# A hybrid decoder layer on one core: the first pair's upper norm factor and seeds earlier, its gate weights split later, the gates' copies one unit later, and the index matrix in another tile

## Chip, core and metric

The kernel runs on one core of one Trainium2 chip. The metric is the device time of one execution in microseconds, the median of several runs. The engines are TensorE (PE, with its weight loads PEld), VectorE (DVE), ScalarE (ACT), GpSimd (POOL) and SyncE (SP); nearly all DMAs are issued by SP, in the order of its queue.

## What is computed

One layer for x of 512 rows by 2048 columns, in float32:

```python
h = rms_norm(x, norm1_g)
proj = h @ w_in            # q, k, v, r of four GLA heads; a rank-16 gate ga; q, k, v of eight dilated heads
gate_pre = ga @ gla_gate_w2 + gla_gate_b
log_g = log_sigmoid(gate_pre) / 16
out_a = gla_mixer(qa, ka, va, ra, log_g)          # chunked gated linear attention
out_b = dilated_mixer(qb, kb, vb, rel_bias)       # three dilated branches, T5 bias by distance
x = x + concat(out_a, out_b) @ w_out
h2 = rms_norm(x, norm2_g)
x = x + (silu(h2 @ w_gate) * (h2 @ w_up)) @ w_down
```

## The kernel before

**Products.** All large matrix products are done as Strassen-like products: two neighbouring 512-column blocks of a weight are a pair, and a pair takes seven products (P1 to P7) of sums of quarters instead of eight. Each operand is split into a high float32r part and a low remainder, and three of the four cross terms are multiplied. For the weights ACT makes the high part (a cast to tile `wh`) and VectorE the low one (a subtraction to `wl`); VectorE also makes the sums of quarters (`wa`, `wb` with `wc`, `wd`). One block is 8 matmuls of 128x512 with the high weight and 4 with the low one; a pair of the input projection has seven products of four blocks, 0 to 27. `wh` and `wl` have two buffers each, the quarters 12, the results that are gathered in SBUF (tag C: seeds and outputs) six, and there are four accumulators and four further PSUM banks.

**The first pair** (q and k of the GLA heads; function `first_pair`) is not left to the scheduler. The string PLAN is a list of tokens, one step each, and the engines execute their instructions in the order of the tokens. The tokens that matter here: `h.k` and `l.k` are the high and low part of weight block k (line 519 on ACT, 527 on VectorE); `mH.k` and `mL.k` (`mH2`, `mL2` for a second result) its high and low matmuls (line 474); `+W.k` a sum of weight quarters (514); `x` scales the transposed input, `+S`, `hi` and `lo` make sums of its quarters and their two parts (494, 504, 208, 211). `sq` squares a half row tile of x with a row sum (681), and `nA.half`, `nB.half`, `nC.half` make the norm factor of the upper (0) or lower (1) 256 rows from these sums: two VectorE instructions (691, 692), a logarithm and an exponential on ACT (694, 695), and three more on VectorE (697 to 699). `seedX.m` copies an accumulator that will be overwritten to a tile of tag C (542), `closeX.m` adds the other part (545), and `sclX.m` multiplies by the norm factor (550); after the second `scl` of a result its two tiles are stored (1065). The results are a, b, c and d: eight tiles, so seedd takes the buffers of seeda after their stores. `gp`, `gh.i` and `gl.i` prepare the rank-16 gate weights: GpSimd sums them (724 to 726), ACT makes the high part (737) and VectorE the low one; `rank` multiplies them (760).

**The next pair** (v of the GLA heads, accumulators at line 402, parts at 373 and 377, sums at 298) goes through Tile's scheduler, with background work: after the matmuls of a block, `step` advances a list of generators by one unit. The first is `gates`, then `bias_tables`; the GLA heads follow when their columns of v are there. In `gates` the 16-row gate product is copied and loaded four times (774, 777), it and the second gate weight are split (779 to 789), and for each of the four row tiles a matmul (795) is scaled and biased by VectorE (797), put through a log-sigmoid (801 to 804) and stored to ls_d (805). `bias_tables` loads a 33x640 matrix of bucket indices in two parts (662), multiplies each with the bias table (664), copies the result (666), stores it (667), and replicates it 128 times in DRAM (669). A `work` tile has one buffer for each tag: a new use of the tag waits until the earlier use has ended. Tag v holds a gate row between 797 and 804, PT the second gate weight, oT the gate bias until the fourth row has read it. A GLA head loads ls_d to T (822), multiplies it for the cumulative sums (833, 834), takes exponentials on ACT (836 to 844), transposes q and k (849), scales them on VectorE (853 to 862), and multiplies them for the scores (873).

Of the kernel before, what the change touches and what calls it, by code (L numbers as in the profile page):

```python
# [20 lines left out]
D = 2048  # L21
# [4 lines left out]
NB = 640  # L26
# [44 lines left out]


PLAN = """
D.r11.3 D.a.3 D.r21.3 D.r12.3 D.c.3 D.r22.3 D.a.0 D.r11.0 D.r11.1 D.a.1 D.a.2 D.r11.2 D.r12.0
D.c.0 D.r12.1 D.r12.2 D.c.1 D.r21.0 D.r22.0 D.b.0 D.c.2 D.r21.1 D.r22.1 D.b.1 D.r22.2 D.r21.2
D.d.0 D.gw D.b.2 x.r11.3.0 x.r11.3.1 hi.A11.3 h.0 lo.A11.3 x.r21.3.0 l.0 mH.0 D.d.1 D.row.0.1
D.row.0.0 D.row.2.0 D.row.1.1 D.row.1.0 D.row.2.1 x.r21.3.1 x.r12.3.1 hi.A21.3 x.r12.3.0 lo.A21.3
h.1 x.r22.3.1 l.1 D.d.2 D.row.3.0 D.row.3.1 D.sm mL.0 hi.A12.3 x.r22.3.0 lo.A12.3 hi.A22.3 +S1.3
x.r11.0.1 mH2.0 x.r11.1.1 lo.A22.3 x.r11.1.0 x.r11.0.0 hi.A11.1 mL2.0 h.2 lo.A11.1 mH.1 hi.A11.0
l.2 x.r11.2.0 x.r11.2.1 mL.1 lo.A11.0 x.r12.0.0 x.r12.0.1 hi.A11.2 mH2.1 hi.A12.0 lo.A11.2  # L80
hi.S1.3 lo.A12.0 x.r12.1.1 mL2.1 lo.S1.3 x.r12.2.0 h.3 +S2.3 mH.2 +S3.3 x.r12.2.1 x.r12.1.0 l.3
hi.A12.2 mL.2 h.4 lo.A12.2 mH.3 hi.A12.1 l.4 x.r21.0.0 x.r22.0.0 +W.8 x.r22.0.1 mL.3 x.r21.0.1
h.5 mH.4 +S1.0 lo.A12.1 x.r21.1.1 hi.S1.0 l.5 mL.4 x.r22.1.0 h.6 lo.S1.0 mH.5 +W.9 x.r22.1.1
x.r21.2.1 x.r22.2.0 l.6 mL.5 x.r22.2.1 h.7 mH.6 gp +S2.0 seeda.0 l.7 x.r21.1.0 seeda.1 mL.6 +W.10
h.8 mH.7 gh.1 +S1.1 hi.S2.0 l.8 x.r21.2.0 hi.S1.1 mL.7 h.9 +S1.2 mH.8 +W.11 hi.S1.2 gh.0 hi.A22.2
lo.S1.1 mL.8 sq.0.1 lo.S1.2 mH.9 l.9 h.10 lo.S2.0 hi.A22.1 sq.1.1 mL.9 +W.12 mH.10 h.11 +S2.1
l.10 hi.S2.1 sq.1.0 l.11 mL.10 h.12 mH.11 lo.S2.1 seedb.0 closea.0 seedb.1 l.12 hi.A22.0 mL.11
sq.3.0 closea.1 mH.12 gl.0 sq.2.1 gl.1 +W.13 hi.S2.3 mL.12 +S2.2 h.14 rank.0 +S3.0 hi.S2.2 l.14
h.13 lo.S2.2 sq.3.1 l.13 sq.0.0 +S4.0 mH.13 hi.S3.0 +S3.2 hi.S4.0 +S3.1 sq.2.0 lo.S4.0 mL.13
+S4.1 h.15 mH.14 +S4.2 hi.S4.1 lo.A22.0 seedc.1 lo.S4.1 mL.14 hi.S4.2 l.15 h.16 mH.15 lo.S4.2  # L90
seedc.0 l.16 mL.15 lo.A22.1 mH.16 lo.A22.2 hi.S3.2 +W.17 mL.16 +W.19 h.17 rank.1 lo.S3.0 lo.S3.2
hi.S3.1 +W.22 l.17 mH.17 +W.18 D.d.3 D.b.3 lo.S3.1 h.18 mL.17 +W.21 h.19 mH.18 l.18 hi.S3.3 l.19
mL.18 mH.19 +W.20 nA.1 h.20 lo.S2.3 mL.19 lo.S3.3 h.21 mH.20 l.20 nB.1 l.21 mL.20 h.22 +S4.3
mH.21 nC.1 l.22 mL.21 h.23 nA.0 mH.22 nB.0 l.23 nC.0 mL.22 h.24 mH.23 scla.0 l.24 scla.1 mL.23
seedd.0 seedd.1 closed.0 mH2.23 closed.1 scld.0 scld.1 mL2.23 h.25 mH.24 hi.S4.3 l.25 lo.S4.3
mL.24 mH2.24 closec.0 closec.1 sclc.0 sclc.1 mL2.24 closeb.1 sclb.1 closeb.0 sclb.0
"""


# [32 lines left out]
def block_kernel(ctx: ExitStack, tc: tile.TileContext, ins, out):  # L132
    nc = tc.nc
    x, w_in, w_out, w_gate, w_up, w_down = (
        ins[n] for n in ("x", "w_in", "w_out", "w_gate", "w_up", "w_down")
    )
# [15 lines left out]
    def nm(s):  # L152
        uid[0] += 1
        return f"{s}_{uid[0]}"
# [499 lines left out]
    def bias_tables():  # L654


        rel = work("T", (33, 8))
        nc.gpsimd.memset(rel[32:33, :], 1.0)
        load(rel[0:32, :], ins["rel_bias"])
        for c0, cn, t0, t1 in ((0, 512, "v", "qT"), (512, NB - 512, "oT", "kT")):  # L660
            oh = work(t0, (33, cn))
            load(oh, ins["onehot"][:, c0 : c0 + cn])
            bp = bank()
            nc.tensor.matmul(bp[:8, :cn], rel, oh, start=True, stop=True)
# [4 lines left out]
        load(rep_d, bass.AP(tensor=bias_d.tensor, offset=0, ap=[[NB, 8], [0, P], [1, NB]]))  # L669
        yield  # L670
# [46 lines left out]
    rank = {}  # L717
# [48 lines left out]
    def gates():  # L766
# [20 lines left out]
        for i in (32, 96):  # L787
            r = slice(i, i + 32)
            nc.vector.tensor_tensor(
                gas[r, :], ga4[r, :], gas[r, :].bitcast(F32), op=ALU.subtract  # L790
            )
        yield
        for t in range(4):
            zp = bank()
# [749 lines left out]
```

## Time and profile before

| | |
|---|---|
| median of three runs | 1941.62 us (1940.41 to 1941.84) |
| the profiled execution | 1938.88 us |
| its span | 1937.1 us |
| granted TensorE clock, mean | 0.999 |
| busy in the span: TensorE, weight loads | 1918.9, 1662.9 us |
| VectorE, ACT, GpSimd | 1650.3, 1094.8, 16.8 us |
| instructions | 25614 |

A row of the timeline gives the start and the length in us, engine, line, operation, result and operands, sizes and the number of instructions merged into it; in brackets stands how long the engine was idle before and what released it. SPq is SP's queue of DMA issues; the length there is that of the issuing, not of the transfer. Ends of matmuls are modelled, and a matmul row overlaps the next one a little.

### The profile page before, as it was taken

The page shows a single profiled execution, that of the slowest core. Times are in us where ns is not written, and L with a number is a line of the kernel's source. Part 1 is how long each engine was busy: PE and PEld are TensorE (multiplying, and loading weights), DVE is VectorE, ACT ScalarE, POOL GpSimd, SP SyncE. Part 2 cuts the span into 40 slices and gives each one's busy share as a digit, 9 for nine tenths or more (in the row PEclk, how much of TensorE's full clock was granted, in tenths as well). Part 3 has the DMA queues.
Part 4 walks back from the last instruction along what each step waited for, and adds up shares of the span by engine and source line. Part 5 has one row for each costly group of instructions (what it writes and reads, how often), then busy time and mean ns, then how long its engine had stood idle before and what let it go on. Part 6 is the DMA issues. An engine that isn't in the chain of part 4 may idle for free.

```text
span 1937.1 us, 25614 instructions
## 1 busy us (share of the span) xinstructions
PE 1918.9 (99%) x9178; PEld 1662.9 (86%) x9178; DVE 1650.3 (85%) x1936; ACT 1094.8 (57%) x1634; POOL 16.8 (1%) x25
## 2 busy tenths in 40 slices
PE   9999999999999999999999999999999999999999
PEld 7888888888888888888888888888888888888887
DVE  8896887778799999878878878878879989989987
ACT  9564564667766675544544545544546646546443
POOL 1000100000000000000000000000000000000000
PEclk9999999999999999999999999999999999999999
DMA  8536555444536564455454454453555865855762
GB/s 337 195 109 220 168 180 173 140 157 146 185 131 208 177 213 130 136 180 161 137 180 156 138 185 142 152 185 122 172 169 175 292 210 184 297 190 180 244 218 66
DMA packets 150360, 345.75 MB, mean 178 GB/s; under 512 B 15494, under 2 KB 42671, under 8 KB 150232
## 3 DMA queue, kind: packets, MB, share of 16 engines
q1 hardware_dynamic: 149944, 343.98, 52.9%
q8 instruction: 72, 1.18, 0.3%
q14 instruction: 56, 0.46, 0.1%
q10 hardware_dynamic: 288, 0.14, 0.0%
HBM read 286.10 MB, written 60.31 MB: 179 GB/s over the span
## 4 chain that ended last, share of the span: by engine, by line
PE 87%; DVE 6%; DMA 4%; issue 2%; ACT 1%; SPq 0%; POOL 0%; DVEq 0%; ACTq 0%; POOLq 0%
PE acc L402 79%; DVE wl L377 2%; PE acc L474 2%; PE bank L1078 1%; PE bank L987 1%; PE bank L963 1%; DVE wa L298 1%; PE bank L980 0%; DVE AS L199 0%; DMA T<-in_xt 0%; DMA k<-in_gw 0%; PE bank L760 0%; DMA wb<-in_w_in 0%; PE bank L954 0%; PE bank L474 0%
## 5 line engine op out<-in xcount | busy, mean ns | idle before, releaser
L402 PE MATMUL acc<-wh,AS 128*128 128x512 f32 x3008 | 711.8, 379 | 0.0
L402 PEld LDWEIGHTS acc<-wh,AS 128*128 128x128 f32 x3008 | 568.2, 189 | 81.2 <-ACT wh L373 0.5
L373 ACT CAST wh<-wa 128x1024 fp32r<-128x1024 f32 x376 | 394.3, 1049 | 396.3 <-PE acc L402 367.6
L402 PE MATMUL acc<-wh,AA 128*128 128x512 f32 x2256 | 534.7, 380 | 0.5 <-ACT wh L373 0.5
L377 DVE TENSOR_TENSOR wl<-wa,wh 128x1024 fp32r<-128x1024 f32 x376 | 456.7, 1217 | 73.0 <-ACT wh L373 47.3
L402 PEld LDWEIGHTS acc<-wh,AA 128*128 128x128 f32 x2256 | 427.1, 189 | 61.7 <-ACT wh L373 0.9
L402 PE MATMUL acc<-wl,AS 128*128 128x512 f32 x1504 | 393.8, 384 | 1.8 <-DVE wl L377 1.6
L402 PEld LDWEIGHTS acc<-wl,AS 128*128 128x128 f32 x1504 | 280.0, 189 | 51.4 <-DVE wl L377 10.2
L402 PE MATMUL acc<-wl,AA 128*128 128x512 f32 x1128 | 296.4, 385 | 0.2
L402 PEld LDWEIGHTS acc<-wl,AA 128*128 128x128 f32 x1128 | 209.9, 189 | 31.4 <-DVE wl L377 2.4
L373 ACT CAST wh<-wb 128x1024 fp32r<-128x1024 f32 x94 | 98.6, 1049 | 123.6 <-PE acc L402 118.9
L373 ACT CAST wh<-wc 128x1024 fp32r<-128x1024 f32 x94 | 98.5, 1048 | 115.9 <-PE acc L402 107.8
L373 ACT CAST wh<-wd 128x1024 fp32r<-128x1024 f32 x94 | 98.6, 1049 | 102.2 <-PE acc L402 98.6
L377 DVE TENSOR_TENSOR wl<-wc,wh 128x1024 fp32r<-128x1024 f32 x94 | 114.5, 1219 | 40.4 <-ACT wh L373 40.4
L377 DVE TENSOR_TENSOR wl<-wd,wh 128x1024 fp32r<-128x1024 f32 x94 | 114.4, 1219 | 36.5 <-ACT wh L373 29.6
L298 DVE TENSOR_TENSOR wa<-wc,wa 128x1024 f32<-128x1024 f32 x94 | 114.4, 1219 | 32.9 <-DMA wc<-in_w_gate 22.1
L377 DVE TENSOR_TENSOR wl<-wb,wh 128x1024 fp32r<-128x1024 f32 x94 | 114.0, 1216 | 5.0 <-ACT wh L373 4.8
L298 DVE TENSOR_TENSOR wa<-wb,wa 128x1024 f32<-128x1024 f32 x94 | 113.6, 1218 | 1.2 <-DMA wb<-in_w_in 0.5
L298 DVE TENSOR_TENSOR wb<-wd,wb 128x1024 f32<-128x1024 f32 x94 | 114.0, 1216 | 0.4
L298 DVE TENSOR_TENSOR wa<-wd,wa 128x1024 f32<-128x1024 f32 x94 | 112.9, 1215 | 0.1
L340 DVE SCALAR_TENSOR_TENSOR seed<-acc,rs,seed 128x512 f32<-128x512 f32 x96 | 70.4, 745 | 29.4 <-PE acc L402 29.3
L324 ACT ACTIVATE seed<-acc,rs 128x512 f32<-128x512 f32 x96 | 60.6, 682 | 5.0 <-PE acc L402 4.9
(320 smaller groups left out, 1315.5 us busy)
## 6 DMA issues: line engine op xcount, KB each, us to landing
wa<-in_w_gate SPq DMA_DIRECT2D x44, 512.0 KB, 3.5
wb<-in_w_up SPq DMA_DIRECT2D x44, 512.0 KB, 4.3
wd<-in_w_up SPq DMA_DIRECT2D x44, 512.0 KB, 4.3
wc<-in_w_gate SPq DMA_DIRECT2D x44, 512.0 KB, 3.5
wa<-in_w_in SPq DMA_DIRECT2D x24, 512.0 KB, 4.6
wc<-in_w_in SPq DMA_DIRECT2D x24, 512.0 KB, 3.5
wb<-in_w_in SPq DMA_DIRECT2D x24, 512.0 KB, 5.4
wd<-in_w_in SPq DMA_DIRECT2D x24, 512.0 KB, 4.4
```

Source lines behind the costliest of these rows:

```text
L298: nc.vector.tensor_tensor(src, other, src, op=ALU.subtract)
L324: nc.scalar.activation(halves(t), unfolded(src[m]), AF.Copy, scale=self.scale(half, m))
L340: nc.vector.scalar_tensor_tensor(halves(seed[m]), unfolded(src[m]), self.scale(half, m), halves(seed[m]), op0=ALU.mult, op1=ALU.add,)
L373: nc.scalar.copy(high[k], sources[k])
L377: nc.vector.tensor_tensor(low[k], sources.pop(k), high[k].bitcast(F32), op=ALU.subtract)
L402: nc.tensor.matmul(p.dst[prod][m], a[:, jj, hl, m * P : (m + 1) * P], folded(w[i][:, jj, :]), start=fresh and g == 0 and i == 0 and jj == ...
L474: recent["pe"] = nc.tensor.matmul(dst[name][m], a[:, jj, hl, m * P : (m + 1) * P], folded(w[:, jj, :]), start=(name, m) not in opened, sto ...
L963: nc.tensor.matmul(lp[:, :n], qh[:, b * P : (b + 1) * P], kh[:, :n], start=True, stop=True)
L987: nc.tensor.matmul(op, vh[:, k, :], lgs[b][:, k * P : (k + 1) * P], start=(k == 0), stop=(k == b))
L1078: nc.tensor.transpose(bk[:, jj, m * P : (m + 1) * P], tiles[m][:, f : f + P], ident)
```

## The change

In PLAN six tokens move and all others keep their order. `gh.1` stood behind mH.7 and stands behind mL.7. `nA.0` now stands behind mL.15, `nB.0` behind h.17, `nC.0` behind lo.S3.1, and `scla.0` and `scla.1` behind h.19; before, these five stood between h.23 and mL.23. The tokens of the lower rows' factor keep their places. In the code:

```diff
-        for c0, cn, t0, t1 in ((0, 512, "v", "qT"), (512, NB - 512, "oT", "kT")):
+        for c0, cn, t0, t1 in ((0, 512, "PT", "qT"), (512, NB - 512, "oT", "kT")):
             oh = work(t0, (33, cn))
...
         gbias = work("oT")
         load(gbias, bass.AP(tensor=ins["gla_gate_b"].tensor, offset=0, ap=[[0, P], [1, 512]]))
+        yield
         ga = work("k", (32, 512))
         nc.scalar.copy(ga, rank["p"][:32, :])
...
                 gas[r, :], ga4[r, :], gas[r, :].bitcast(F32), op=ALU.subtract
             )
         yield
+        yield
         for t in range(4):
```

So in `gates` the copies come one unit later and the four row tiles two. Lines behind 772 have a number one or two higher in the changed kernel.

ACT near the end of the first pair, before: the rows behind the two casts of blocks 18 and 19 (wh from wb), up to the copies seedd (seed_992 and seed_994); seed_520 and seed_525 are seeda, and rs_105 is the value between Ln and Exp.

```order
L519 CAST wh_870<-wb_271 128x1024
L208 CAST AS_132_882<-xT_114 128x2x256
L519 CAST wh_901<-wa_240 128x1024
L519 CAST wh_909<-wa_244 128x1024
...
L519 CAST wh_972<-wd_858 128x1024
L550 ACTIVATE seed_520<-seed_520,rs_102 128x512
L550 ACTIVATE seed_525<-seed_525,rs_102 128x512
L542 COPY seed_992<-acc_412 128x512
L542 COPY seed_994<-acc_413 128x512
```

The same place in the changed kernel:

```order
L519 CAST wh_877<-wb_271 128x1024
L550 ACTIVATE seed_520<-seed_520,rs_102 128x512
L550 ACTIVATE seed_525<-seed_525,rs_102 128x512
L208 CAST AS_132_893<-xT_114 128x2x256
...
L519 CAST wh_960<-wb_864 128x1024
L519 CAST wh_976<-wd_862 128x1024
L542 COPY seed_992<-acc_412 128x512
L542 COPY seed_994<-acc_413 128x512
```

The two scalings of seeda have moved ahead of six casts, and the copies seedd now follow the cast of block 24 at once.

VectorE from the third gate row to the fourth (tile v, line 797 before, 799 after), before: wl is a low split, a row to wa or wb a sum of quarters, L the end of a gate row.

```order
L797 SCALAR_TENSOR_TENSOR v_1219<-bank_1217,rs_102,oT_1081 128x512
L377 TENSOR_TENSOR wl_1301<-wa_1028,wh_1296 128x1024
L298 TENSOR_TENSOR wa_1099<-wd_1320,wa_1099 128x1024
L377 TENSOR_TENSOR wl_1323<-wa_1066,wh_1318 128x1024
L804 SCALAR_TENSOR_TENSOR L_1221<-v_1219,L_1221 128x512
L377 TENSOR_TENSOR wl_1341<-wa_1099,wh_1339 128x1024
L797 SCALAR_TENSOR_TENSOR v_1248<-bank_1246,rs_102,oT_1081 128x512
```

The same stretch in the changed kernel:

```order
L799 SCALAR_TENSOR_TENSOR v_1257<-bank_1255,rs_102,oT_1081 128x512
L666 COPY qT_1324<-bank_1322 8x512
L377 TENSOR_TENSOR wl_1340<-wa_1089,wh_1338 128x1024
L298 TENSOR_TENSOR wb_1161<-wd_1271,wb_1161 128x1024
L806 SCALAR_TENSOR_TENSOR L_1259<-v_1257,L_1259 128x512
L377 TENSOR_TENSOR wl_1357<-wd_1213,wh_1355 128x1024
L799 SCALAR_TENSOR_TENSOR v_1288<-bank_1286,rs_102,oT_1081 128x512
```

The copy qT of the bias table's first part has come into this stretch, and low splits that stood in it now stand further ahead. Counted from the pair's first sum of quarters (line 298), 20 rows of 128x1024 stand ahead of the fourth gate row before and 23 now; the narrow rows ahead of it are the same but for that copy.

SP from the small part of the index matrix (oT from in_onehot) to the first va stores, before: wc are the pair's third quarters, bias_d and rep_d the bias table and its replication, T the loads for the first GLA head.

```order
L662 DMA oT_1285<-in_onehot 33x128
L259 DMA wc_1481<-in_w_in 128x1024
L805 DMA ls_d_121<-L_1250 128x512
L662 DMA v_1278<-in_onehot 33x512
L259 DMA wc_1499<-in_w_in 128x1024
L259 DMA wc_1519<-in_w_in 128x1024
...
L259 DMA wc_1538<-in_w_in 128x1024
L669 DMA rep_d<-bias_d 1024x1x640
L1065 DMA va_124<-seed_1383 128x512
L1065 DMA va_124<-seed_1401 128x512
```

In the changed kernel:

```order
L259 DMA wc_1481<-in_w_in 128x1024
L662 DMA oT_1327<-in_onehot 33x128
L259 DMA wc_1499<-in_w_in 128x1024
...
L259 DMA wc_1519<-in_w_in 128x1024
L824 DMA T_1553<-ls_d_120 128x128
L669 DMA rep_d<-bias_d 1024x1x640
L1067 DMA va_124<-seed_1383 128x512
L1067 DMA va_124<-seed_1401 128x512
L259 DMA wc_1538<-in_w_in 128x1024
```

The small part of the index matrix now stands behind the first wc load, the large part (to PT) far ahead of this stretch, and the fourth wc load behind the replication and two stores.

TensorE's rows of the first GLA head move too: the cumulative sums of lines 833 and 834 stand around the high part of block 23 of the pair, the transposes behind that of block 25 and the scores behind that of block 26; before, all but one sum stood behind block 27. From the second GLA head's sums on every engine has its old order.

More of the change, by code (lines that the diff above doesn't have):

```diff
@@ L73 @@
 PLAN = """
[L74 to L85, printed above, removed]
@@ L92 @@
[L92 to L96, printed above, removed]
+D.r11.3 D.a.3 D.r21.3 D.r12.3 D.c.3 D.r22.3 D.a.0 D.r11.0 D.r11.1 D.a.1 D.a.2 D.r11.2 D.r12.0 D.c.0
@@ L97 @@
++W.20 nA.1 h.20 lo.S2.3 mL.19 lo.S3.3 h.21 mH.20 l.20 nB.1 l.21 mL.20 h.22 +S4.3 mH.21 nC.1 l.22
+mL.21 h.23 mH.22 l.23 mL.22 h.24 mH.23 l.24 mL.23 seedd.0 seedd.1 closed.0 mH2.23 closed.1 scld.0
+scld.1 mL2.23 h.25 mH.24 hi.S4.3 l.25 lo.S4.3 mL.24 mH2.24 closec.0 closec.1 sclc.0 sclc.1 mL2.24
+closeb.1 sclb.1 closeb.0 sclb.0
 """
```

24 lines of the change are left out of this document (18 added, 6 removed).

## The prediction

> **What bounds the kernel now.** I read the page's busy shares first, then TensorE's waits, then the timelines of all engines around each wait that the change can reach.
>
> ```profile
> span 1937.1 us, 25614 instructions
> PE 1918.9 (99%) x9178; PEld 1662.9 (86%) x9178; DVE 1650.3 (85%) x1936; ACT 1094.8 (57%) x1634; POOL 16.8 (1%) x25
> ```
>
> TensorE works for 1918.9 of 1937.1 us, so only its 18.2 us of idle time can be won by moving instructions. The change touches the first 200 us of the span. TensorE's waits from 80 to 180 us, as total, times and longest:
>
> ```profile
> PE acc L474 <- ACT seed L542: 2.0, 1, 2.0
> PE bank L873 <- DVE qT L857: 1.5, 1, 1.5
> PE bank L795 <- DVE gas L789: 0.6, 1, 0.6
> ...
> PE bank L664 <- DMA v<-in_onehot: 0.4, 1, 0.4
> ```
>
> These are 4.5 us, and with the waits near 40 us below they are all that the change can reach. Behind 200 us the order of every engine is the old one; TensorE then works almost without a gap, so what is won or lost before comes out at the end undiminished.
>
> **Later split of the gate weights (gh.1).** ACT, DVE and TensorE around it:
>
> ```profile
> 33.92 0.35 ACT L737 CAST gs<-v 128x192 fp32r<-128x192 f32 x1 [1.47 <-POOL v L726]
> 35.24 0.69 DVE L504 TENSOR_TENSOR kT<-kT,PT 128x512 f32<-128x512 f32 x1 [0.28 <-ACT kT L494]
> 37.72 1.78 PE L474 MATMUL acc<-wh,AS 128*128 128x512 f32 x7 [0.52 <-DVE AS L211]
> 42.93 1.13 PE L474 MATMUL acc<-wl,AS 128*128 128x512 f32 x4 [0.62 <-DVE wl L527]
> 50.03 1.23 DVE L527 TENSOR_TENSOR wl<-wd,wh 128x1024 fp32r<-128x1024 f32 x1 [0.20 <-ACT wh L519]
> ```
>
> ACT stands 1.47 us at L737 for GpSimd, with two casts and a scaling queued behind. With these ahead of it, VectorE's sum at 35.24 loses its 0.28 us wait (0.35 with the restart), and the two TensorE waits that follow end that much sooner, but no more, because VectorE ends them. ACT gains about 0.9 us of its 1.47, which also takes away the 0.20 at 50.03. So VectorE is 0.35 us early near 43 us and 0.55 after 50.
>
> **Earlier norm of the upper rows (nA, nB, nC).** VectorE gets two small instructions earlier, and then three:
>
> ```profile
> 43.00:80.00 37.00, 36.74 (x198) 32.71 (x199) 36.66 (x51) 24.89 (x40) 1.01 (x2) 1.00 0.47 163
> 67.56 1.22 DVE L514 TENSOR_TENSOR wb<-wd,wb 128x1024 f32<-128x1024 f32 x1
> 68.89 2.00 ACT L519 CAST wh<-wb 128x1024 fp32r<-128x1024 f32 x2 [3.46 <-PE acc L474]
> 69.99 2.00 PE L474 MATMUL acc<-wh,AS 128*128 128x512 f32 x8 [0.26 <-ACT wh L519]
> 70.43 2.35 DVE L527 TENSOR_TENSOR wl<-wb,wh 128x1024 fp32r<-128x1024 f32 x2
> 71.82 1.03 PE L474 MATMUL acc<-wl,AS 128*128 128x512 f32 x4
> 73.83 0.15 DVE L691 TENSOR_REDUCE xms<-ss 128x2 f32<-128x4 f32 x1
> 74.09 1.29 DVE L211 TENSOR_TENSOR AS<-xT,AS 128x512 fp32r<-128x512 f32 x2
> 78.17 0.15 DVE L697 SCALAR_TENSOR_TENSOR nrs<-xms,rs 128x2 f32<-128x2 f32 x1
> 78.63 1.22 DVE L527 TENSOR_TENSOR wl<-wa,wh 128x1024 fp32r<-128x1024 f32 x1
> ```
>
> The first row gives, behind the length, the busy time of TensorE, its weight loads, VectorE, ACT and GpSimd: VectorE is busy for 36.66 of 37 us, so an instruction put in delays all behind it. From start to start nA costs 74.09 - 73.83 = 0.26 us, nC 78.63 - 78.17 = 0.46. The waits on them: the subtraction at 67.56 ends at 68.78, the cast follows 0.11 later, and TensorE's 0.26 us wait at 69.99 is for that cast. (The row names PE, whose high part ended at 68.86 as well; I take the DVE.) The low split at 70.43 ends at 71.65, and TensorE needs it at 71.82: 0.17 us of room. With 0.72 us put in and 0.55 brought along, the split ends 0.17 us later than before, which just uses up that room, and the restart of the matmuls adds some 0.1. **Both edits together: +0.1 us**; -0.35 if TensorE's old slack covers it, +0.4 if the 0.20 is not won. The same five instructions are taken out behind 79 us, where VectorE waits anyway. ACT's two nB instructions lie in an ACT gap.
>
> **Earlier scaling and store of the first seeds (scla).**
>
> ```profile
> 83.33 1.34 ACT L550 ACTIVATE seed<-seed,rs 128x512 f32<-128x512 f32 x2
> 84.07 0.94 SPq L1065 DMA_DIRECT2D qa<-seed  x2
> 87.17 1.22 ACT L542 COPY seed<-acc 128x512 f32<-128x512 f32 x2 [2.51 <-DMA qa<-seed]
> 84.77 1.03 PE L474 MATMUL acc<-wl,AA 128*128 128x512 f32 x4
> 87.81 2.19 PE L474 MATMUL acc<-wh,AA 128*128 128x512 f32 x8 [2.02 <-ACT seed L542]
> ```
>
> Eight seed tiles share six buffers, so the copies seedd reuse seeda's, whose stores to qa go out at 84.07 and free them at 87.1. TensorE waits for that copy, because the next block overwrites the accumulator that it reads. Now scla follows the two casts of 68.89, at about 71, and with 1.3 us of scaling and 3.1 from issue to copy the buffers are free about 75. ACT reaches the copies at 83.3, where the scalings were, and ends both at 84.6; TensorE arrives at 87.81 - 2.02 = 85.8. The wait is gone, with the matmul restart **-2.1 us** (2.0 by the wait alone). What is late next on ACT is nothing: it waits for TensorE. On SP the two stores now stand ahead of nine weight loads; their user is the next pair, which comes behind all the seeds, so a few us there cost nothing.
>
> **Gate copies later, index matrix in another tile.**
>
> ```profile
> 107.86 0.48 PE L795 MATMUL bank<-w2s,gas 128*128 128x512 f32 x1 [0.60 <-DVE gas L789]
> 126.30 0.74 DVE L797 SCALAR_TENSOR_TENSOR v<-bank,rs,oT 128x512 f32<-128x512 f32 x1
> 131.50 0.32 SPq L662 DMA_DIRECT2D v<-in_onehot  x1
> 132.19 1.67 PE L402 MATMUL acc<-wh,AS 128*128 128x512 f32 x7
> 134.23 1.02 PE L664 MATMUL bank<-v,T 33*8 33x512 f32 x2 [0.36 <-DMA v<-in_onehot]
> kT<-k SPq DMA_DIRECT2D x4, 64.0 KB, 2.0
> wc<-in_w_in SPq DMA_DIRECT2D x4, 512.0 KB, 3.5
> ```
>
> The first gate matmul now stands a block and a half later, behind gas: 0.6 us gone. The large part of the index matrix goes to PT, free after w2s near 103 us, and its matmul near 123 us waits for nothing. But the small part stays in oT, which holds the gate bias until the fourth gate row (126.30) has read it. That row now has three more wide VectorE instructions (1.13 us each, from 2.35 - 1.22) and a copy (0.6) ahead: it starts at 126.30 + 4.0 = 130.3 and ends at 131.05. The load can only then be issued. If it takes as long as v's (131.50 to 134.23, 2.73 us), its matmul starts at 133.8. TensorE is there at 132.19 - 0.6 + 1.0 (the large pair, moved ahead) + two matmuls (0.45) = 133.0: **a new wait of 0.8 us** for DMA oT<-in_onehot. Before, the pairs started at 134.23 with both still to do and one high matmul behind; now with the small one (0.3) and six high ones. That is 133.8 - 134.23 + 0.2, so **the gain of both edits is only 0.2 us**. With kT's 2.0 it is 0.9; with a landing 1 us later it is a loss of 0.8.
> The Trainium skill, "DMA: Bandwidth & Descriptors", section "Queues, rings and completion order", says that each DMA engine takes descriptors in ring order; a 512 KB wc load is issued some 0.7 us ahead of oT's, and by that rule the small part lands with it, about 134, and the sum is 0.2 us worse. That 2.73 stands against 2.0 here agrees with it.
>
> **The first GLA head.**
>
> ```profile
> 173.04 1.27 ACT L622 ACTIVATE cout<-acc,rs 128x512 f32<-128x512 f32 x2 [4.78 <-PE acc L402]
> 175.28 0.42 DVE L853 SCALAR_TENSOR_TENSOR qT<-bank,L 128x256 f32<-128x256 f32 x1 [5.77 <-ACT L L838]
> 177.12 0.29 PE L873 MATMUL bank<-qT,kT 128*64 128x128 f32 x1 [1.50 <-DVE qT L857]
> ```
>
> Before, its cumulative sums, transposes and scores stand in one row behind the pair's last block, and ACT's exponentials wait behind cout. In the changed order the sums stand at block 23 of the pair, the transposes in 25, the scores in 26, each with matmuls between, and the exponentials ahead of cout. VectorE's chain from L853 to the scores (177.12 - 175.28 = 1.8 us) then lies beside a low and a high part (1.0 and 1.8). The wait goes: **-1.6 us** (1.5 by the row; 0 if another wait takes its place). Its inputs are ready: the fourth gate row is stored some 5 us later, but the last load of T stands behind the same va stores as before.
>
> **Sum**: 0.1 - 2.1 - 0.2 - 1.6 = -3.8 us on the profiled execution's 1938.88 us (1.78 around the span), 1935.1. The three timed runs' median, 1941.62, lies 2.7 above it; the same step gives **1937.8**. A measurement of this kernel can tell about 0.2%, 3.9 us, from no change, so the forecast lies on the edge.
>
> **Rivals.**
> - *The index part lands early.* For it speaks kT's 2.0 us; against it the wc load just ahead. With -0.9 there and -0.35 at the start: -4.9, 1936.7.
> - *The GLA head's wait comes back.* Block 26 needs L857 in time, and VectorE has the wide splits between. Against it: VectorE idled 5.77 us there. Then -2.2: 1939.4.
> - *The seed copy still waits*, for a store held up behind a weight load on SP, so that the change doesn't do what it says. The stores take 3.1 us and now have 12. Then -1.7: 1939.9.
> - *Slower: the pair's fourth wc load.* It was issued ahead of the 2560 KB replication and is now behind it and two stores:
>
> ```profile
> 139.31 0.73 SPq L669 DMA_DIRECT2D rep_d<-bias_d  x1
> 156.63 1.05 ACT L373 CAST wh<-wc 128x1024 fp32r<-128x1024 f32 x1 [1.54 <-PE acc L402]
> DMA to landing us min/median/max: 2.1/5.0/10.9
> ```
>
> The last row is the landing of the va stores, 10.9 us for one issued behind the replication. Issued at 144.7, the load would land at 155.6, ahead of its cast at 156.63; TensorE itself has room until about 158.8. Past 14 us every us is lost on TensorE, and past 18 us the kernel is slower than before; at 20 us it takes 1943.8. By the same ring rule of the Trainium skill the load ends behind the replication on the engines that both use, and the trace's 10.9 agrees.
>
> **Chances.** Forecast 0.50 (1937.2 to 1938.4), index part early 0.22, GLA wait back 0.18, seeds still wait 0.06, late weight load 0.04. Faster by over 0.2%: 0.22 and 0.22 of the forecast, 0.44; same: 0.28 + 0.18 + 0.06 + 0.02 = 0.54; slower 0.02. The range takes in the first three and the edge of the fourth: 1936.2 to 1939.9.
>
> **What would show it.** TensorE's wait for L542 gone and qa's stores issued about 72; a wait below 0.4 us at the low part near 72; no wait for gas, and about 0.8 for oT<-in_onehot; none at L873. A wait at the cast of wc near 157, a seed copy that waits for DMA, or a landing of oT under 2.2 us would prove the steps wrong.

## The result and the profile after

Each kernel was timed in turn with the kernel before on the same chip. The changed kernel took **1937.35 us** (median of 12 runs, 1934.61 to 1941.00) against 1941.63 (12 runs, 1939.28 to 1944.06): ratio 0.9982, 95% interval 0.9974 to 0.9990. A second timing gave 0.9986 (0.9976 to 0.9996), 1938.51 against 1941.54 us. So the change makes the kernel faster by 0.14 to 0.18%, some 3 us; both intervals lie below 1. The forecast was 1937.8 us in a range of 1936.2 to 1939.9.

The page of the changed kernel seems to say the opposite: this one execution is longer than the profiled one of before (span 1937.1, TensorE busy 1918.9).

```profile
span 1939.2 us, 25621 instructions
PE 1921.1 (99%) x9178; PEld 1662.6 (86%) x9178; DVE 1650.4 (85%) x1936; ACT 1094.8 (56%) x1634; POOL 16.0 (1%) x25
```

It took 1941.00 us, the longest of its twelve runs. TensorE's waits in its first 200 us (total, times, longest) say why:

```profile
PE acc L474 <- ACT wh L519: 4.1, 3, 2.9
...
PE bank L664 <- DMA oT<-in_onehot: 0.7, 1, 0.7
PE acc L402 <- ACT wh L373: 0.5, 1, 0.5
...
PE acc L474 <- DVE wl L527: 0.2, 1, 0.2
```

All the waits that the prediction took away are gone: L542, the scores (now L875), gas, v<-in_onehot. The new one for oT is there, 0.7 us against 0.8 forecast. But one of 2.9 us stands near 40 us, where nobody looked for it. The timeline of the same run, the places of the prediction in order:

```profile
75.67 0.93 SPq L1067 DMA_DIRECT2D qa<-seed  x2
76.33 1.13 PE L474 MATMUL acc<-wl,AS 128*128 128x512 f32 x4 [0.21 <-DVE wl L527]
87.94 1.07 ACT L542 COPY seed<-acc 128x512 f32<-128x512 f32 x2
132.43 0.73 DVE L799 SCALAR_TENSOR_TENSOR v<-bank,rs,oT 128x512 f32<-128x512 f32 x1
133.19 0.32 SPq L662 DMA_DIRECT2D oT<-in_onehot  x1
135.94 0.38 PE L664 MATMUL bank<-oT,T 33*8 33x128 f32 x2 [0.72 <-DMA oT<-in_onehot]
160.41 1.05 ACT L373 CAST wh<-wc 128x1024 fp32r<-128x1024 f32 x1 [3.38 <-DMA wc<-in_w_in]
174.04 0.32 PE L875 MATMUL bank<-qT,kT 128*64 128x128 f32 x1
202.79 1.05 PE L835 MATMUL bank<-mats,T 128*128 128x128 f32 x8
```

The stores to qa leave twelve us ahead of the copies, which wait for nothing. The small index part is loaded as soon as the fourth gate row (132.43 to 133.16) has read oT, and its matmul starts 2.75 us after the issue (2.73 in the forecast). The scores start without a wait. The last row, the second GLA head's sums, is the first place where all later orders agree; it stood at 202.42 before:

```profile
202.42 1.05 PE L833 MATMUL bank<-mats,T 128*128 128x128 f32 x8
```

This run had lost 3.65 us by L760's first matmul (52.73 against 49.08) and made up all but 0.37 of it by this row. A second profile of the same program has no such loss (first run below), and shows the change alone.

### The profile page after: what moved, and what is told of

It is laid out like the page before. It is cut to its first block, busy times and chain, and to the rows that moved or that the text cites. A ratio compares the mean times of both kernels' runs of the same rounds, so it can differ in the third digit from the quotient of the medians.

```text
span 1939.2 us, 25621 instructions
## 1 busy us (share of the span) xinstructions
PE 1921.1 (99%) x9178; PEld 1662.6 (86%) x9178; DVE 1650.4 (85%) x1936; ACT 1094.8 (56%) x1634; POOL 16.0 (1%) x25
## 4 chain that ended last, share of the span: by engine, by line
PE 83%; DVE 8%; DMA 4%; issue 3%; ACT 1%; POOL 0%; SPq 0%; DVEq 0%; ACTq 0%; POOLq 0%
PE acc L402 77%; DVE wl L377 3%; PE bank L1080 1%; DVE wa L298 1%; PE bank L989 1%; PE bank L965 1%; PE acc L474 1%; DVE AS L199 1%; PE bank L982 0%; DMA wc<-in_w_gate 0%; DMA T<-in_xt 0%; PE bank L474 0%; DMA wb<-in_w_in 0%; POOL v L724 0%; DMA k<-in_gw 0%
## 5 line engine op out<-in xcount | busy, mean ns | idle before, releaser
L402 PE MATMUL acc<-wh,AS 128*128 128x512 f32 x3008 | 711.8, 379 | 0.0
L402 PEld LDWEIGHTS acc<-wh,AS 128*128 128x128 f32 x3008 | 568.1, 189 | 81.1 <-ACT wh L373 0.5
L402 PE MATMUL acc<-wh,AA 128*128 128x512 f32 x2256 | 533.6, 379 | 0.5 <-ACT wh L373 0.5
L402 PEld LDWEIGHTS acc<-wh,AA 128*128 128x128 f32 x2256 | 426.1, 189 | 61.5 <-ACT wh L373 1.2
L402 PE MATMUL acc<-wl,AS 128*128 128x512 f32 x1504 | 394.5, 385 | 2.9 <-DVE wl L377 2.9
L402 PEld LDWEIGHTS acc<-wl,AS 128*128 128x128 f32 x1504 | 279.6, 189 | 54.6 <-DVE wl L377 12.5
L402 PE MATMUL acc<-wl,AA 128*128 128x512 f32 x1128 | 296.4, 385 | 0.6 <-DVE wl L377 0.4
L402 PEld LDWEIGHTS acc<-wl,AA 128*128 128x128 f32 x1128 | 209.6, 189 | 32.4 <-DVE wl L377 3.2
L373 ACT CAST wh<-wc 128x1024 fp32r<-128x1024 f32 x94 | 98.5, 1048 | 117.2 <-PE acc L402 105.7
```

The source lines that it names most:

```text
L373: nc.scalar.copy(high[k], sources[k])
L402: nc.tensor.matmul(p.dst[prod][m], a[:, jj, hl, m * P : (m + 1) * P], folded(w[i][:, jj, :]), start=fresh and g == 0 and i == 0 and jj == ...
```

## The experiments

Each was timed in five rounds beside the kernel before, whose median was 1940.2 to 1941.5 us in these timings. Four marks are read from each profile: the length of GpSimd's first copy of the gate weights, the start of L760's first matmul, what the place of L542 costs (from the low part ahead of it to the second high part behind it, over the 3.45 us that this takes undisturbed), and the stretch from the last low part of L474 to the second head's sums, which holds the gates, the index matrix and the first GLA head.

| kernel | median us | ratio (95%) | GpSimd copy | L760 at | L542 costs | stretch |
|---|---|---|---|---|---|---|
| before | 1941.6 | | 1.34 | 49.08 | 2.5 | 107.4 |
| changed | 1937.4 | 0.9982 (0.9974-0.9990) | 7.36 | 52.73 | 0 | 105.6 |
| e5 changed, again | 1938.5 | 0.9986 (0.9976-0.9996) | 1.41 | 48.75 | 0 | 105.9 |
| e1 norm alone | 1939.0 | 0.9991 (0.9981-1.0001) | 0.29 | 50.00 | 0 | 107.5 |
| e2 split alone | 1941.1 | 1.0004 (0.9995-1.0013) | 1.13 | 48.79 | 4.5 | 108.2 |
| e3 index tile alone | 1940.4 | 0.9993 (0.9982-1.0003) | 0.68 | 49.25 | 5.0 | 105.7 |
| e4 steps alone | 1943.9 | 1.0019 (1.0008-1.0029) | 4.97 | 51.77 | 4.2 | 110.6 |
| e6 changed, no steps | 1938.4 | 0.9983 (0.9973-0.9993) | 7.05 | 51.29 | 0 | 106.0 |
| e7 changed, small part in k | 1938.8 | 0.9987 (0.9977-0.9997) | 1.48 | 48.70 | 0 | 106.7 |
| e8 changed, no GpSimd | 1936.3 | 0.9975 (0.9966-0.9984) | none | 49.50 | 0 | 105.8 |
| e9 before, no GpSimd | 1939.8 | 0.9996 (0.9987-1.0005) | none | 49.44 | 4.6 | 107.6 |
| e10 no GpSimd, one step | 1936.5 | 0.9977 (0.9968-0.9987) | none | 48.91 | 0 | 105.2 |
| e11 as e10, old split | 1936.5 | 0.9978 (0.9969-0.9988) | none | 49.84 | 0 | 105.3 |
| e12 changed, old split | 1936.6 | 0.9982 (0.9973-0.9991) | 0.95 | 49.78 | 0 | 106.0 |

Behind the stretch, from the second head's sums to the end of the span, the profiles take 1733.4 to 1737.4 us (before 1734.7, changed 1736.4, again 1734.8). This scatter of 4 us in a part whose order is the same everywhere is why single executions can't be compared by their spans. In three of the profiles (before, e1, e9) the granted clock falls once in this part too, to 0.66 to 0.68 over the 5 us behind a wait of 1.6 to 1.9 us that ends at 552 to 556 us.

**e5: the changed kernel again.** No edit.

> The changed kernel itself once more, for a second profile of it. In its first profile GpSimd's first copy of the gate weights takes 7.36 us and TensorE waits 2.85 us near 40 us; in the five other profiles that copy takes 0.3 to 5.0 us and ends 0.14 us behind an end of VectorE's row of instructions. My theory: the copy waits until VectorE pauses, and whether it comes just before or just after the start of a VectorE instruction is a matter of chance, so that a second profile may show it short; then there is no wait near 40 us and the first matmul of L760 stands at 48.8 to 50.5 us in place of 52.7. Rival: the later split of the gate weights makes it long each time; then this profile shows over 5 us again. The waits behind 60 us are those of the first profile: 0.6 and 0.2 near 74 us or less, 0.7 for oT<-in_onehot, none at L542 and the scores.

```profile
30.41 1.41 POOL L724 COPY v<-k 128x128 f32<-128x128 f32 x1 [28.87 <-DMA k<-in_gw]
69.59 1.99 PE L474 MATMUL acc<-wh,AS 128*128 128x512 f32 x8 [0.18 <-ACT wh L519]
71.80 1.13 PE L474 MATMUL acc<-wl,AS 128*128 128x512 f32 x4 [0.21 <-DVE wl L527]
131.70 0.38 PE L664 MATMUL bank<-oT,T 33*8 33x128 f32 x2 [1.01 <-DMA oT<-in_onehot]
198.55 1.05 PE L835 MATMUL bank<-mats,T 128*128 128x128 f32 x8
```

GpSimd's copies have the lengths of the profile before, so the two can be laid side by side: the second head's sums come at 198.55 in place of 202.42, **3.87 us earlier**, where the sum of the prediction was 3.8. The long copy isn't there every time; the rival falls.

**e1: the norm alone.** All of the plan's moves but gh.1.

```diff
-h.23 nA.0 mH.22 nB.0 l.23 nC.0 mL.22 h.24 mH.23 scla.0 l.24 scla.1 mL.23
+l.16 mL.15 nA.0 ... h.17 nB.0 ... lo.S3.1 nC.0 h.18 ... h.19 scla.0 scla.1 mH.18
```

> The kernel before with the norm tokens of the upper rows and the two scalings moved as in the change (nA, nB, nC, scla), and nothing else. My theory: TensorE's wait for the seed copy of L542 (2.0 us) is gone and the first stores to qa are issued near 72 us; the two instructions of nA and the three of nC cost VectorE 0.72 us near 72 us, and without the later split of the gate weights there is no lead to pay it from, so TensorE's wait for the cast near 70 us grows from 0.26 to about 0.5 and a wait of about 0.3 stands at the low part behind it. From the first matmul of L760 to the first scores' values (L885) that is +0.6 - 2.1 = -1.5 us, 0.1% of the whole. Rival: VectorE had slack there that the rows do not show; then no wait grows near 70 us and the stretch is 2.1 us or more shorter. Second rival: the copy still waits for a store that stands behind weight loads on SP; then L542 keeps over 1 us.

```profile
72.38 0.93 SPq L1065 DMA_DIRECT2D qa<-seed  x2
73.04 1.13 PE L474 MATMUL acc<-wl,AS 128*128 128x512 f32 x4 [0.21 <-DVE wl L527]
```

The wait for L542 goes with this edit alone; the low part behind nA and nC waits 0.21 us. The longer wait for the cast near 70 us that I expected isn't there: from L760 to the low part ahead of L542 it takes 36.09 us in place of 35.69, 0.4 more where I had 0.6. The ratio is 0.9991. The interval takes in 1, so the time alone doesn't tell this edit from nothing; the profile shows the place.

**e2: the split alone.** Of the plan's moves only gh.1.

```diff
-h.8 mH.7 gh.1 +S1.1 hi.S2.0 l.8 x.r21.2.0 hi.S1.1 mL.7 h.9
+h.8 mH.7 +S1.1 hi.S2.0 l.8 x.r21.2.0 hi.S1.1 mL.7 gh.1 h.9
```

> The kernel before with the second cast of the gate weights (gh.1) moved behind mL.7, and nothing else. My theory: ACT's wait for GpSimd falls from 1.47 us to about 0.6 if GpSimd's first copy takes 1.3 us as in the profile of before, the two TensorE waits near 37 and 43 us shrink by 0.35 us together, and nothing else moves: 0.3 us, not to be told from no change in the whole. If GpSimd's copy takes 7.4 us, as in the profile of the changed kernel, ACT waits some 3.7 us and TensorE 2.9 us, in either order of the tokens. Rival: the 2.9 us wait at 40 us in the changed kernel's profile comes from the move itself; then this run shows it with a short GpSimd copy, and the kernel is 2 us slower.

L760 starts 0.29 us earlier than before, and the kernel as a whole doesn't differ. With a copy of 1.1 us the move makes no wait, so its rival falls too.

**e3: the index matrix in another tile, and no later gates.**

```diff
-        for c0, cn, t0, t1 in ((0, 512, "v", "qT"), (512, NB - 512, "oT", "kT")):
+        for c0, cn, t0, t1 in ((0, 512, "PT", "qT"), (512, NB - 512, "oT", "kT")):
```

> The kernel before with the large part of the index matrix in the tile PT in place of v, and nothing else: no later gate copies. My theory: the order of the instructions already shows the first GLA head spread over several blocks in this kernel, so its wait at L873 (1.5 us) goes with this line alone, 1.4 to 1.6 us; the wait for the index matrix (0.36 us) goes too, since the bias tile is read by the fourth gate row at 126.3 us and the small part lands near 130 us; the wait for gas (0.6 us) stays. Together 1.8 us shorter from the gate matmuls to L885. Rival: the head needs the later gates as well, and a wait of 1 us or more stands at the scores for L or qT. Second rival: the small part waits for a landing of 5 us or more, and TensorE stands there over 0.5 us.

```profile
110.22 0.47 PE L795 MATMUL bank<-w2s,gas 128*128 128x512 f32 x1 [0.60 <-DVE gas L789]
131.02 0.38 PE L664 MATMUL bank<-oT,T 33*8 33x128 f32 x2
174.30 0.32 PE L873 MATMUL bank<-qT,kT 128*64 128x128 f32 x1
```

This one word does it: the stretch falls from 107.4 to 105.7 us, as in the whole change. The wait for gas stays; that for oT doesn't arise, since the fourth gate row reads it 4.3 us earlier than in the changed kernel, counted from the last low part of L474. The whole kernel, 0.9993, can't be told from no change.

**e4: the two steps alone**, with the index matrix in v.

```diff
         load(gbias, bass.AP(tensor=ins["gla_gate_b"].tensor, offset=0, ap=[[0, P], [1, 512]]))
+        yield
...
         yield
+        yield
         for t in range(4):
```

> The kernel before with the two added steps in the gates and nothing else: the index matrix stays in v. My theory: the wait for gas (0.6 us) goes, the tile v is free only after the fourth gate row, 4 us later than before, so the pair of index matmuls waits for its load as before or up to 1 us longer (0.4 to 1.4 us), and the GLA head stays in one row with its wait of 1.5 us. Together between 0.3 us shorter and 0.5 us longer: no change. Rival: the later steps are what spreads the GLA head; then L873 has no wait and the stretch is 1.5 to 2 us shorter.

```profile
144.64 1.01 PE L664 MATMUL bank<-v,T 33*8 33x512 f32 x2 [2.31 <-DMA v<-in_onehot]
```

Worse than I allowed: 0.19% slower. The wait for gas goes, but v is free only after the fourth gate row, which now stands 4.5 us later, so TensorE waits 2.3 us for the index matrix. Behind this wait the granted clock is 0.66 over 5 us, and the stretch is 3.2 us longer. I expected the 1.5 us at the scores to stay; it is 0.15 there and 0.86 at a cast just ahead. The steps can stand only together with the other tile.

**e6: the changed kernel without the two steps.**

```diff
         load(gbias, bass.AP(tensor=ins["gla_gate_b"].tensor, offset=0, ap=[[0, P], [1, 512]]))
-        yield
...
         yield
-        yield
         for t in range(4):
```

> The changed kernel without the two added steps in the gates: the norm, the split and the index tile stay. My theory: the gate copies and rows stand as before and their wait for gas (0.6 us) comes back, the wait of the small index part for oT (0.7 us) goes, and the GLA head stays spread. From the end of the last L474 matmuls to the second head's sums it takes within 0.2 us of the changed kernel (105.6 us), as the run with the index tile alone did (105.7). So the two steps are worth nothing. Rival: they gain by themselves; then this stretch is 0.5 us or more longer and the whole slower by as much.

106.0 against 105.6 and 105.9 us for the stretch, and 0.9983 for the ratio: as the changed kernel. Beside the new tile the steps are worth nothing; they trade 0.6 us for gas against 0.7 to 1.0 for oT. By chance this profile has the long copy again, 7.05 us.

**e7: the small index part in a tile that is free sooner.**

```diff
-        for c0, cn, t0, t1 in ((0, 512, "PT", "qT"), (512, NB - 512, "oT", "kT")):
+        for c0, cn, t0, t1 in ((0, 512, "PT", "qT"), (512, NB - 512, "k", "kT")):
```

> The changed kernel with the small part of the index matrix in the tile k in place of oT, which is free once the four copies of ga are made. My theory: TensorE's wait of 0.72 us for oT<-in_onehot goes, and nothing takes its place before 140 us: 0.7 us shorter. But the 2560 KB replication is now issued before all four wc loads of the pair, near 128 us: by the rival of the prediction (slower) these land behind it, 155 us or later for loads that are cast from 149 us on, and TensorE waits 2 us or more for a wc cast; then the kernel is slower than the changed one by 1 to 5 us.

```profile
126.52 0.72 SPq L669 DMA_DIRECT2D rep_d<-bias_d  x1
140.96 1.88 SPq L259 DMA_DIRECT2D wc<-in_w_in  x4
152.11 1.13 PE L402 MATMUL acc<-wl,AA 128*128 128x512 f32 x4 [1.38 <-DVE wl L377]
```

The wait for oT goes, and the prediction's slower rival takes its place in small: the four wc loads stand behind the replication and two stores, are issued at 141 us, and TensorE waits 1.4 and 0.2 us for what is made of them. The stretch is 0.8 us longer than in e5, and the whole is the same within the interval.

**e8: GpSimd out of the gate weights.**

```diff
-            nc.gpsimd.tensor_copy(kinds[:, 0], gv[:, :, 0])
-            nc.gpsimd.tensor_copy(kinds[:, 1], gv[:, :, 1])
-            nc.gpsimd.tensor_tensor(kinds[:, 2], gv[:, :, 1], gv[:, :, 0], op=ALU.subtract)
+            nc.scalar.copy(kinds[:, 0], gv[:, :, 0])
+            nc.scalar.copy(kinds[:, 1], gv[:, :, 1])
+            nc.vector.tensor_tensor(kinds[:, 2], gv[:, :, 1], gv[:, :, 0], op=ALU.subtract)
```

> The changed kernel with the three preparing instructions of the gate weights on ACT (the two copies, about 0.3 us each) and VectorE (the subtraction, about 0.3 us) in place of GpSimd. My theory of the port: in the changed kernel GpSimd waits for a pause of VectorE, and in some runs ACT, VectorE and TensorE then wait in turn for it, some 3 us of TensorE near 40 us. Here nobody can wait for it: L760 starts at 48.5 to 50.5 us in every profile, the slow group of runs near 1941 us is gone, and the median is 0.5 to 1.5 us below that of the changed kernel. Rival: the long copy in the changed kernel comes from GpSimd itself (its first instruction of that kind) and only shows by chance with VectorE's pause; that rival gives the same time here, and is told from mine by the ends of the copies, not by this run. Second rival: 0.6 us more on ACT and 0.3 on VectorE cost TensorE as much as the wait, and the median is the same.

What it rests on are the ends of GpSimd's copies. First the changed kernel's first profile:

```profile
31.11 7.36 POOL L724 COPY v<-k 128x128 f32<-128x128 f32 x1 [29.56 <-DMA k<-in_gw]
37.63 0.69 DVE L211 TENSOR_TENSOR AS<-xT,AS 128x512 fp32r<-128x512 f32 x1
39.23 0.35 ACT L737 CAST gs<-v 128x192 fp32r<-128x192 f32 x1 [3.74 <-POOL v L726]
41.09 0.69 DVE L211 TENSOR_TENSOR AS<-kT,AS 128x512 fp32r<-128x512 f32 x1 [2.77 <-ACT AS L208]
40.58 3.16 PE L474 MATMUL acc<-wh,AS 128*128 128x512 f32 x8 [2.85 <-ACT wh L519]
```

The copy starts while VectorE works without a pause, and ends at 38.47 us, 0.15 behind VectorE's 38.32. VectorE stops there because it needs ACT, ACT stands at L737 for GpSimd, and GpSimd has been waiting for VectorE to stop. In e4, where the split stands at its old place, VectorE runs dry earlier, at the sum of kT, and the same happens after 5 us (end 35.26, VectorE's end 35.12):

```profile
30.29 4.97 POOL L724 COPY v<-k 128x128 f32<-128x128 f32 x1 [28.75 <-DMA k<-in_gw]
33.90 1.22 DVE L527 TENSOR_TENSOR wl<-wa,wh 128x1024 fp32r<-128x1024 f32 x1
37.35 0.69 DVE L504 TENSOR_TENSOR kT<-kT,PT 128x512 f32<-128x512 f32 x1 [2.23 <-ACT kT L494]
```

And in e12 VectorE pauses at 32.32 us for a weight load, and the copy is over at 32.47:

```profile
31.52 0.95 POOL L724 COPY v<-k 128x128 f32<-128x128 f32 x1 [29.98 <-DMA k<-in_gw]
31.10 1.22 DVE L527 TENSOR_TENSOR wl<-wc,wh 128x1024 fp32r<-128x1024 f32 x1
32.82 1.47 DVE L514 TENSOR_TENSOR wa<-wb,wa 128x1024 f32<-128x1024 f32 x1 [0.50 <-DMA wb<-in_w_in]
```

A pause isn't always needed. In the kernel before the copy also ends 0.15 us behind an end of VectorE (31.73 against 31.58), but VectorE goes on at 31.65:

```profile
30.39 1.34 POOL L724 COPY v<-k 128x128 f32<-128x128 f32 x1 [28.84 <-DMA k<-in_gw]
30.36 1.22 DVE L527 TENSOR_TENSOR wl<-wc,wh 128x1024 fp32r<-128x1024 f32 x1
31.65 1.23 DVE L514 TENSOR_TENSOR wa<-wb,wa 128x1024 f32<-128x1024 f32 x1
```

The same holds in e5 and e7 (1.41 and 1.48 us). What lets the copy in behind one instruction there, and keeps it waiting through nine in the changed kernel's first profile, the runs don't show.

Where VectorE stands idle (e1) the copy takes 0.29 us. A slow first instruction of GpSimd would not end 0.14 to 0.15 us behind VectorE's row each time, nor take 0.29 as first instruction of its kind in e1; that rival is out. The Trainium skill, "SBUF — State Buffer", section "SBUF: two separate sides", states the rule: GpSimd shares its port to the memory with VectorE's second one, and a GpSimd instruction that reads there and a VectorE instruction with two inputs from there lock each other out for a whole instruction; it gives about 115 ns from VectorE's end, and the traces agree with 0.14 to 0.15 us. It speaks of one instruction; the 7.36 us copy waited through nine, and the measurement decides.

Without GpSimd all eleven runs lie between 1935.0 and 1938.1 us. The changed kernel's 24 lie in two groups, 15 from 1934.1 to 1938.3 and 9 from 1939.8 to 1941.6. The high group is gone, and 1936.3 is the lowest median of the study, 2.2 us below the changed kernel in the same timing; its ratio lies below, but the intervals overlap. That the nine high runs had the long copy is likely and not shown: one of them is profiled (1941.00 us, 7.36), one low run has the short copy (1935.10, 1.41), and e6's profile has the long one in a run of 1938.65 us, between the groups.

**e9: the kernel before without GpSimd.** The three lines of e8 in the kernel before, nothing else:

```diff
-            nc.gpsimd.tensor_copy(kinds[:, 0], gv[:, :, 0])
+            nc.scalar.copy(kinds[:, 0], gv[:, :, 0])
...
```

> The kernel before, with only the three preparing instructions of the gate weights moved from GpSimd to ACT and VectorE. My theory: the lottery at the gate weights is in the kernel before too, so its spread shrinks here as it did for the changed kernel (from 7.4 to 3.1 us between the fastest and the slowest run), and its median falls by 0.5 to 2 us, to about 1940. The waits of the prediction all stand: 2 us or more for L542, 0.6 for gas, 0.4 or more for v<-in_onehot, 1.5 for the scores. Against it the changed kernel without GpSimd (1936.3) then shows what the change is worth with the lottery taken out of both: 3.5 to 5 us. Rival: only the later split makes the long copies, so that the kernel before has nothing to gain here; then the median stays at 1941 to 1941.5.

The median falls by 1 us, which the interval can't tell from nothing; the spread falls from 6.1 (1937.6 to 1943.7, 24 runs) to 4.2 us (11 runs). This pair, e9 and e8, gives the change with GpSimd out of both: 0.9975 against 0.9996, some 4 us. By the second head's sums the two profiles lie 5.57 us apart (204.70 and 199.13), more than the 3.8 of the rows of before; behind them e8 takes 2.07 us longer, within the scatter of that part. Why it is more is seen at L542. First the timeline of TensorE in e9:

```profile
84.82 1.03 PE L474 MATMUL acc<-wl,AA 128*128 128x512 f32 x4
88.25 3.15 PE L474 MATMUL acc<-wh,AA 128*128 128x512 f32 x8 [2.40 <-ACT seed L542]
91.19 1.80 PE L474 MATMUL acc<-wl,AA 128*128 128x512 f32 x4
```

Then the busy times from 84 to 92 us of TensorE, its weight loads, VectorE, ACT and GpSimd, with the granted clock as third number from the end. In e9:

```profile
84.00:92.00 8.00, 5.60 (x19) 4.06 (x18) 2.06 (x3) 3.81 (x7) 0.00 (x0) 0.83 0.73 246
```

The same stretch of the kernel before:

```profile
84.00:92.00 8.00, 5.98 (x27) 4.66 (x26) 2.88 (x4) 4.76 (x8) 0.00 (x0) 1.00 0.69 239
```

And of the changed kernel's second profile (e5), which has no wait there:

```profile
84.00:92.00 8.00, 8.00 (x39) 7.01 (x38) 4.92 (x7) 3.79 (x6) 0.00 (x0) 1.00 0.54 189
```

A high part of e5 in this stretch:

```profile
85.71 1.89 PE L474 MATMUL acc<-wh,AA 128*128 128x512 f32 x8
```

In e9 the granted clock is 0.83 over these 8 us, and eight matmuls behind the wait for L542 take 3.15 us in place of 1.89. So the wait costs 4.6 us, not 2.4. The same stands in e2, e3 and e4 (4.2 to 5.0 us). The profile of before is the one of five with this order in which the clock stayed at 1.00. In all nine profiles without the wait it is 1.00 here.

**e10: without GpSimd, and with only the second step.**

```diff
         load(gbias, bass.AP(tensor=ins["gla_gate_b"].tensor, offset=0, ap=[[0, P], [1, 512]]))
-        yield
```

> The changed kernel without GpSimd and with only the second of the two added steps in the gates (the one ahead of the four gate rows). My theory: gas is made where the kernel before made it and its matmul stands one unit later, so there is no wait for gas; the fourth gate row reads oT one unit sooner than in the changed kernel, its small index part is loaded some 2 to 3 us sooner, and the wait of 0.7 to 1.0 us for it goes. From the last L474 matmuls to the second head's sums it takes 104.9 to 105.1 us in place of 105.8, and the median is 0.7 us below that without GpSimd alone (1936.3), so 1935.6. Rival: the small part stays late since it waits for weight loads on SP and not for oT; then the wait stays.

```profile
124.34 0.32 SPq L662 DMA_DIRECT2D oT<-in_onehot  x1
125.95 0.38 PE L664 MATMUL bank<-oT,T 33*8 33x128 f32 x2 [0.28 <-DMA oT<-in_onehot]
```

The wait for gas is gone, and that for oT falls to 0.3 us: the stretch is 0.5 us shorter than in e8. The median, 1936.5, does not show it; half a us is below what these runs resolve. With no weight load just ahead of it the small part takes 1.6 us from issue to matmul, against 2.75 in the changed kernel.

**e11: as e10, with the split at its old place.**

```diff
-h.8 mH.7 +S1.1 hi.S2.0 l.8 x.r21.2.0 hi.S1.1 mL.7 gh.1 h.9
+h.8 mH.7 gh.1 +S1.1 hi.S2.0 l.8 x.r21.2.0 hi.S1.1 mL.7 h.9
```

> As the run with one step, and the second cast of the gate weights (gh.1) back at its place of before, behind mH.7. My theory: without GpSimd ACT waits for nothing there, so the place of the split decides nothing: L760's first matmul stands within 0.3 us of the same start, and the median is the same within 0.4 us. Rival: the split matters by itself, because it stands on ACT ahead of two casts that VectorE waits for; then TensorE waits 0.3 us longer near 37 us.

The median is the same. L760 comes 0.9 us later in this profile (49.84 against 48.91), but TensorE is 1.06 us late by 32 us already (31.90 against 30.84), ahead of the split. The main part is a wait of 0.7 us for a cast, which e10 doesn't have; it comes from a load of kT for which ACT stood 1.5 us. The split adds nothing to it.

**e12: the changed kernel with the split at its old place.** The same edit on the changed kernel itself:

```diff
-h.8 mH.7 +S1.1 hi.S2.0 l.8 x.r21.2.0 hi.S1.1 mL.7 gh.1 h.9
+h.8 mH.7 gh.1 +S1.1 hi.S2.0 l.8 x.r21.2.0 hi.S1.1 mL.7 h.9
```

> The changed kernel with GpSimd as it was, and only gh.1 back at its place of before, behind mH.7. In the changed kernel's 24 timed runs 15 lie between 1934.1 and 1938.4 and 9 between 1939.8 and 1941.6. My theory: the high group is the long GpSimd copy. With the split later VectorE runs dry 2.4 us later (it then stands at the sum of AS, before at the sum of kT), so that the copy takes 7 us in place of 5 and TensorE waits 2.85 us in place of 1.9. With the split back the low group stays and the high one moves down by 0.5 to 1.5 us or loses members: the median is 0.3 to 1.5 us below that of the changed kernel (1937.4 and 1938.5 in its two timings). If the profile has the long copy, it takes at most 5.2 us. Rival: the place of the split decides nothing, or saves 0.35 us when the copy is short, as the prediction had it; then the median is the same or 0.3 us higher, and a high group as large as before stays near 1940.7.

All eleven runs lie between 1934.7 and 1939.5 us, two of them (1939.2 and 1939.5) in the gap between the groups and none in the high one; at 9 in 24 that would come about once in 180 such series (0.625 to the power of 11). But the kernel before was itself lower in this timing (1940.2 us) than in the two of the changed kernel (1941.6 and 1941.5), by 1.3 us or more, and with 1.3 us added these two would lie in the high group. The ratio to the kernel before is 0.9982, as for the changed kernel, and this profile shows a short copy (0.95 us). That a long copy is dearer with the later split, the profiles show: 7.36 and 7.05 us, with TensorE waiting 2.85 and 2.84 us, against 4.97 and 1.95 in e4. Whether long copies come more often with it isn't shown: two of five profiles with the later split have one, one of five with the old place.

## Why the prediction was right, step by step

The terms are read from e5 against the profile before, which have nearly equal GpSimd copies.

- **Split and norm, +0.1 us.** L760 comes at 48.75 in place of 49.08, -0.33 (-0.35 forecast); the low part ahead of L542 at 84.85 in place of 84.77, +0.08. The 0.21 us wait at the low part near 72 us is the one forecast at below 0.4. That the first figure agrees so well is in part luck: without a long copy L760 comes at 48.70 to 49.50 us in the five profiles with the later split and at 49.08 to 50.00 in the six without, and with GpSimd out the split gains nothing (49.50 in e8, 49.44 in e9).
- **Seeds, -2.1 us.** Measured -2.5 against this one profile, and -4.2 to -5.0 against four others with the old order. The mechanism was right (e1 alone shows it), the size too small: I priced the wait and one restart, and not the clock that follows, which the profile at hand happened to keep. This is the step that was mis-sized.
- **Gates and index, -0.2 us.** Behind the index matmuls a high part of L402 starts at 149.81 us in place of 152.11. Counted from the last low part of L474 (92.62 and 95.02) that is 0.1 us lost; in the first profile 0.19 is won. The new wait was 0.7 and 1.0 us (0.8 forecast). That these two edits nearly cancel each other was right, e3 and e6 show it from both sides, and e4 shows that the steps alone cost 3.2 us.
- **The first GLA head, -1.6 us.** Measured 1.57 in both profiles. What the prediction didn't say is that the index tile alone spreads the head. Over more profiles this term and the one before hold together: the stretch takes 107.65 us in the mean of four with the old order (before, e1, e2, e9) and 105.83 in four with the changed one (changed, e5, e8, e12), 1.8 us less, as forecast.
- **Rivals.** The early index part, the late seed copies and the GLA wait didn't come. The late weight load nearly did. The prediction named a wait at the cast of wc near 157 us as a sign that its steps are wrong, and that wait came: in the first profile ACT stands for the fourth wc load (160.41 us, 1.8 behind the rhythm of the casts; 0.6 behind it in e5). The load was issued at 148.29 us and its cast came 12.1 us later, where the prediction had 10.9 and a landing ahead of the cast. The room that it gave TensorE held, though: TensorE takes the block up at 162.41 without a wait. In e7 the late loads show.

The whole agreed to within half a us of 1937.8 in the first timing and 0.7 in the second, but not for the reasons of the sum alone. Two terms that I left out point in opposite directions, and as far as they cancel in the medians, that is luck. The clock behind L542's wait makes the change worth 2 us more than the profile showed. GpSimd's lottery, the copy whose length differs from run to run, puts L760 at 51.29 to 52.73 us in the three profiles with a long copy, in place of 48.70 to 50.00. The prediction held that only 0.2% can be told from no change and gave "faster" by more than that 0.44; at 0.14 to 0.18% the result falls on its other side, "same" at 0.54, though the intervals, about 0.1% to either side, are narrower than it thought. The prediction read ACT's 1.47 us wait for GpSimd as a fixed length; it is between nothing and 3.7 us. What stays open: whether the move of gh.1 makes that worse (e12), and whether a part of the gain is given back behind 200 us; the stretch from the second head's sums to the end is 1.1 us longer in the mean of the profiles with the early norm (1735.6 us, nine) than in those without (1734.5, five), in a scatter of 4 us.

The lowest ratio is that of the changed kernel without GpSimd (e8; with one step less, e10): 0.9975 of the kernel before, with a spread of 3.1 us (11 runs) against 8.0 of the kernel before in the same timing (34 runs). Its interval overlaps that of the changed kernel. Of the change itself it should need only the norm and the one tile name; no run has just these two.

## What to carry to other kernels

Before a wait is priced from one profile, look at what follows it: the time up to the next undisturbed part, and the granted clock there, not the idle time alone; a second profile of the same program shows which waits have a fixed length. A GpSimd copy beside a VectorE that works without pause had no length of its own here (1.34 to 7.36 us): where VectorE's pause hangs on it through a third engine, a short copy becomes the longest wait of its stage. Where a tile is reused, its name alone can decide in which block a later stage stands, so try the names apart from the steps.

## What the runs showed of the hardware that was not expected

GpSimd's 128x128 copy took 0.29 us beside an idle VectorE, and beside a busy one 1.34 to 1.48 (before, e5, e7) or 4.97 to 7.36 us (e4, e6, changed). VectorE in turn was slowed once GpSimd had got in (1.47 in place of 1.22 us for the 128x1024 sum at 32.82 in e12). Behind the first 20 us of the fourteen profiles TensorE waits 1.83 to 2.87 us ten times, and in eight of these cases its clock fell: the granted clock was then 0.66 to 0.68 over 5 us, and matmuls of 128x512 took up to twice as long for about 3 us. After 2.84 us in e6 and 2.02 in before it did not fall; after shorter waits it fell twice, behind 1.77 us in before and 1.58 in e9, both past 550 us. The Trainium skill, "TensorE: Matmul & The Clock Gate", section "What's actually happening", has the clock halved after an idle window of about 3.4 us that runs free of the program; that it depends on where in such a window the wait falls agrees with the eight of ten, but the drops here came after shorter waits, and the measurement decides.
